# Hybrid attention and PEER block, 1 core: U and V rows gathered together, one-hot rows in groups of two

## Chip, cores and metric

One core of one Trainium2 chip runs the whole program. The metric is the device time of one execution in microseconds.

## Reference

One layer for 512 tokens of width 1024: a projection, latent attention and gated linear attention with an output projection, and then the part that the change is in, a retrieval from 16384 single-neuron experts (PEER):

```python
q = (hf @ w_q).reshape(T, PH, 2, PEER_HALF)
scores = jnp.einsum('thpd,hpnd->thpn', q, sub_keys, preferred_element_type=jnp.float32)
s, idx = lax.top_k(scores, K)
...
best, pos = lax.top_k(cand, K)
expert = jnp.take_along_axis(cand_idx, pos, axis=-1)
gate = jax.nn.softmax(best, axis=-1)
...
u = jnp.take(u_tab, eb, axis=0)
a = jax.nn.gelu(jnp.einsum('td,thkd->thk', xb, u, preferred_element_type=jnp.float32), approximate=False)
c = (a * gb).astype(h.dtype)
return jnp.einsum('thk,thkd->td', c, jnp.take(v_tab, eb, axis=0))
```

Each token picks 8 heads x 16 = 128 experts. It takes the dot product with each expert's row of U, a GELU and the gate, and the sum of the rows of V weighted by that.

## The kernel before

Products are made from fp32r halves: every operand x is split into hi (ScalarE copies it) and lo (x - hi, on DVE or POOL), and three matmuls hi*hi, lo*hi, hi*lo make one product.

The 512 tokens go two ways through the experts.

**The dense way, tokens 128 to 511 (ND = 384).** The 16384 experts are 128 blocks ("experts" below) of 128. For each of them the kernel makes U x (24 matmuls of 384 columns: 8 pieces of the width, three halves each), a GELU, a weight per expert and token (0 where the token did not pick it), and then C V (18 matmuls of 512 columns: 3 token blocks, 2 halves of the width, three halves each) into six PSUM banks. The weight comes from one-hot rows: `route(tt)` finds the picks of 128 tokens; `onehot(o)` builds for 8 tokens, on DVE and in f16, for each token a 128x128 row of ones at the first index (x1) and of the gate's hi and lo half at the second index (xh, xl); `spread(o)` multiplies them, two f16 matmuls per token, and ScalarE evicts them to `gs`, which goes to DRAM (`gd`) every 32 tokens. In the tiles x1, xh and xl of `[128, 2, 128, 4]` the innermost index is the token in a group of four, so the 128 columns of one token are four elements apart.

**The gathered way, tokens 0 to 127 (GT = 128).** One token per partition. For each of the 128 picks an indirect DMA on POOL's queue brings that token's row of U (4 KB), DVE takes the dot product in one pass (`scalar_tensor_tensor` with `accum_out`), after 32 picks ScalarE makes the GELU, and the rows of V are brought and added to `gout` in one DVE pass each. `gather()` is a generator of 256 steps that the other loops call.

**What sets the order.** The program runs in the order in which it is written; each engine takes its own instructions in that order. While `route` and `onehot` run on DVE, a planner fills TensorE with up-matmuls of the next experts. `Metered` adds a cost in ns for each instruction of PE and DVE, and `fill()` (L1187) calls `some(1)`, an eighth of an expert's up-matmuls, as long as PE's sum is behind DVE's. `gathered(G1)`, `gathered(GO)`, `gathered(GC)` advance the gather. Experts made so early go through DRAM (`gx` to `gad`, and back as `ga`); those that are left (`fresh`) are made between the steps of the down loop (L1383: `down`, `c_hi`, `v_hi`, `up_out`, `weigh`, `c_lo`, `v_lo`, `refill`, `up`, `gathering`) and stay in SBUF (`gf`). The lo half of a weight tile (wlo) is made by `lo_home[0]`, first POOL, and DVE from L952 on.

Of the kernel before, what the change touches and what calls it, by code (L numbers as in the profile page):

```python
# [10 lines left out]
F32 = mybir.dt.float32  # L11
# [11 lines left out]
D = 1024  # L23
# [8 lines left out]
NEG = -3.0e38  # L32
NA = 6
NF = 6
XAT = 120
# [4 lines left out]
P15 = 8  # L40
G1, GO = 0.25, 0.75
LEAD = 3000.0
# [9 lines left out]
ND = T - GT  # L52
GSL = 32
GC = 0.25
GBUF = 5
LEAVE = 8
# [38 lines left out]
def layout(x, positions, g_mix, w_in, g_q_lat, w_qb, g_kv_lat, w_kvb, w_a2, b_a2, g_gla, w_branch_a,  # L95
# [39 lines left out]
    a["u"] = ct(peer_u[0].reshape(128, 128, NC_D, 128).transpose(0, 3, 2, 1))  # L135
    a["ur"] = ct(peer_u[0])
    a["v"] = ct(peer_v[0].reshape(128, 128, D))
# [54 lines left out]
@with_exitstack
def body(ctx, tc, a, out):
# [757 lines left out]

    lo_home[0] = dve  # L952
    some(P15)
    product_keys(15)
    some(3 * NC_D - P15)
    ax = ExitStack()
    for tt in range(NT):
# [27 lines left out]
    gact = gp.tile([128, 128], F32, name="gact")  # L985
    NSB = 128 // GSL
    gsteps = [256]

    def gather():
        rows = {}  # L990
        src = [a["ur"], a["v"].rearrange("a b d -> (a b) d")]
        batches = [(0, 0)] + [x for b in range(NSB) for x in ([(0, b + 1)] if b + 1 < NSB else []) + [(1, b)]]
        work = [(v, GSL * b + j) for v, b in batches for j in range(GSL)]

        def fetch(n):
            if n < len(work):
                v, j = work[n]
                rows[n] = gp.tile([128, D], F32, name="rows", bufs=GBUF)
                pool.indirect_dma_start(out=rows[n], out_offset=None, in_=src[v],  # L999
                                        in_offset=bass.IndirectOffsetOnAxis(ap=gidx[:, j:j + 1], axis=0))  # L1000

        for n in range(GBUF - 2):
            fetch(n)
        yield
        for n, (v, j) in enumerate(work):
            fetch(n + GBUF - 2)
            r = rows.pop(n)
            gsteps[0] -= 1
            if v == 0:
                dve.scalar_tensor_tensor(r, r, 1.0, hrep, op0=OP.mult, op1=OP.mult, accum_out=gact[:, j:j + 1])  # L1010
                if j % GSL == GSL - 1:
                    b = slice(j + 1 - GSL, j + 1)
                    act.activation(gact[:, b], gact[:, b], AF.Gelu)
                    dve.tensor_tensor(gact[:, b], gact[:, b], ggat[:, b], op=OP.mult)
            else:
                dve.scalar_tensor_tensor(gout, r, gact[:, j:j + 1], gout, op0=OP.mult, op1=OP.add)
            yield
# [14 lines left out]
    NS = PH * TOPK  # L1032
    i1T, i2T, gh, gl = [pr.tile([128, T], F16, name=n) for n in ("i1T", "i2T", "gh", "gl")]
    TB = 32
    gd = dr.tile([128, T // TB, 128, TB], F32, name="gd")
    GS = 2.0 ** 15
    def route(tt):
# [4 lines left out]

        kx = pr.tile([128, 2, TOPK, PH, TOPK], F16, name="kx")
        d1 = pr.tile([128, PH, TOPK], F16, name="d1")
# [11 lines left out]
        pos = pr.tile([128, PH, TOPK], U32, name="pos")  # L1056
        wk = pr.tile([128, PH, NCAND], F32, name="cand2")
        for op in range(5):
            for hd in range(PH):
                x, y, b, i8 = cand[:, hd], wk[:, hd], best[:, hd], pos[:, hd]  # L1060
                if op == 0:
                    dve.max(b[:, 0:8], x)
                elif op == 1:
                    dve.max_index(i8[:, 0:8], b[:, 0:8], x)
                elif op == 2:
                    dve.match_replace(y, b[:, 0:8], x, NEG)
                elif op == 3:
                    dve.max(b[:, 8:16], y)
                else:
                    dve.max_index(i8[:, 8:16], b[:, 8:16], y)  # L1070
                if hd % 4 == 3:
                    if (op, hd) == K1:
                        act.activation(kx[:, 0], d1.rearrange("p h a -> p a h")[:, :, :, None].to_broadcast(spread_k), AF.Copy)
                    if (op, hd) == K2:
                        act.activation(kx[:, 1], fi[:, :, 1].rearrange("p h a -> p a h")[:, :, :, None].to_broadcast(spread_k), AF.Copy)
                    yield
# [7 lines left out]
        dve.tensor_copy(pf, pos.rearrange("p h k -> p (h k)"))  # L1084
        ge = pr.tile([128, TOPK, NS], F16, name="ge")
        m = pr.tile([128, 2, TOPK, NS], F16, name="m")
# [4 lines left out]
        def flat(x):  # L1091
            return x.rearrange("p a h k -> p a (h k)")

# [5 lines left out]
        dve.tensor_tensor(g, g, sm[:, 1, :, None].to_broadcast([128, PH, TOPK]), op=OP.mult)  # L1099
        dve.tensor_tensor(m[:, 0], ge, flat(kx[:, 0]), op=OP.mult)  # L1100
        yield
# [11 lines left out]
        yield  # L1113
        dve.tensor_tensor(m[:, 0], ge, flat(kx[:, 1]), op=OP.mult)
        n = TOPK // 2
        while n > 1:
            dve.tensor_tensor(m[:, 0, :n], m[:, 0, :n], m[:, 0, n:2 * n], op=OP.add)
            n //= 2
        yield
        dve.tensor_tensor(e2, m[:, 0, 0], m[:, 0, 1], op=OP.add)  # L1120
        for _ in range(6):
            yield
        if tt == 0:
# [3 lines left out]
            return  # L1127
        ts = slice(tt * 128, (tt + 1) * 128)
        p = pmm()
# [10 lines left out]
    def onehot(o):  # L1140

        full = [128, 2, 128, 4]
        it = iota[:, None].to_broadcast(full)
        t0 = 8 * o

        def col(x):
            return x[:, t0:t0 + 8].rearrange("p (g t) -> p g t", t=4)[:, :, None, :].to_broadcast(full)

        e1, e2, eh, el = [pr.tile([128, 2, 128, 4], F16, name=n, bufs=XB) for n in ("x1", "x2", "xh", "xl")]
        dve.tensor_tensor(e2, it, col(i2T), op=OP.is_equal)  # L1150
        (pool if o % 4 in PSH else dve).tensor_tensor(el, e2, col(gl), op=OP.mult)
# [27 lines left out]
    iota = pr.tile([128, 128, 4], F16, name="iota")  # L1179
    act.activation(iota, cc(C_IOTA, 128)[:, :, None].to_broadcast([128, 128, 4]), AF.Copy)  # L1180
    step = pr.tile([128, TOPK, NS], F16, name="step")
# [201 lines left out]
    for n in range(128 - ENDS):  # L1383
# [58 lines left out]
```

## Time and profile before

| | |
|---|---|
| median of 3 runs | 1702.72 us (1697.27 to 1703.1) |
| profiled execution, its own time | 1697.78 us |
| its span | 1695.9 us |
| PE busy | 1655.2 us, 8505 matmuls |
| DVE, ACT, POOL busy | 1263.6, 679.0, 575.9 us |
| DMA | 406.25 MB, 240 GB/s over the span |
| mean granted clock of TensorE | 0.993 |

The stages by time: projections, attention and the routing projection up to about 545 us; routing of the first tokens up to 632 us; one-hot products with up-matmuls beside them up to 905 us; the last early experts up to 950 us; the down loop up to 1657 us; the final norm up to the end. Matmuls are pipelined and overlap in the profile, so the time that one costs is the distance from its start to the next one's start. The granted clock is a share of full speed, 2.4 GHz; 0.50 is 1.2 GHz. Helpers record most operations under one line (L162), so groups are told apart by the names of the tiles, `out<-in`.

### The profile page before, as it was taken

What the parts mean: (1) busy time and instruction counts of PE and PEld (TensorE: products, weight loads), DVE (VectorE), ACT (ScalarE), POOL (GpSimd) and SP (SyncE); (2) the same over time, 40 slices, a digit from 0 to 9 for tenths busy, and PEclk for the clock granted to TensorE, in tenths of its full rate; (3) what the DMA queues carried; (4) which work ended last, traced back from release to release, by engine and by line L of the source; (5) the groups of instructions that cost most, each with busy time, mean ns of one, the idle gap of its engine ahead of it and who ended that gap; (6) DMA issues with size and microseconds to landing.
All of it is one profiled execution on the core that took longest, in us unless ns stands there. A gap on an engine that the chain in (4) does not pass through costs nothing.

```text
span 1695.9 us, 23253 instructions
## 1 busy us (share of the span) xinstructions
PE 1655.2 (98%) x8505; PEld 1445.6 (85%) x8505; DVE 1263.6 (75%) x2535; ACT 679.0 (40%) x999; POOL 575.9 (34%) x362
## 2 busy tenths in 40 slices
PE   7999999999998999999999999999999999999998
PEld 5777657888877999999999988888888888888887
DVE  6725575254889988989894677877788788878885
ACT  5442544244223635454444433333333333333333
POOL 4532233445330111111111243443454443454550
PEclk9999999999998999999999999999999999999999
DMA  5222113434232777787889999999999999999993
GB/s 173 66 74 72 52 67 132 141 130 149 88 100 88 250 242 235 262 274 260 278 299 344 330 313 325 324 338 328 305 371 331 341 365 328 319 364 324 336 332 131
DMA packets 168849, 406.25 MB, mean 240 GB/s; under 512 B 13383, under 2 KB 86216, under 8 KB 167072
## 3 DMA queue, kind: packets, MB, share of 16 engines
q1 hardware_dynamic: 118624, 230.09, 39.8%
q0 software_dynamic: 37008, 134.58, 22.8%
q10 hardware_dynamic: 13104, 40.11, 6.4%
q8 instruction: 66, 1.08, 0.3%
q14 instruction: 47, 0.39, 0.1%
HBM read 357.28 MB, written 47.45 MB: 239 GB/s over the span
## 4 chain that ended last, share of the span: by engine, by line
PE 85%; DVE 9%; issue 2%; ACT 2%; DMA 2%; POOL 0%; SPq 0%; DVEq 0%; POOLq 0%; ACTq 0%
PE pmm L162 54%; PE pk L162 17%; PE pst L162 14%; DVE kd L162 3%; DVE la L162 2%; DVE tmp L162 2%; DVE rB L162 1%; DMA raw<-in_w 1%; DMA gad<-gx 0%; DMA ga<-gad 0%; DVE r L162 0%; POOL wlo L241 0%; DVE act_lo L162 0%; ACT act_hi L322 0%; DVE stat L162 0%
## 5 line engine op out<-in xcount | busy, mean ns | idle before, releaser
L999 POOL DMA_INDIRECT rows<-in_ur,gidx x128 | 170.0, 1328 | 547.0 <-DVE rows L162 445.4
L162 PE MATMUL pmm<-act_hi,whi 128*128 128x384 f32 (+1 forms) x832 | 303.4, 365 | 12.0 <-ACT act_hi L327 8.7
L162 PE MATMUL pmm<-act_hi,wlo 128*128 128x384 f32 (+1 forms) x832 | 294.9, 354 | 8.5 <-DVE wlo L162 8.5
L162 PE MATMUL pmm<-act_lo,whi 128*128 128x384 f32 (+1 forms) x832 | 294.7, 354 | 0.5 <-DVE act_lo L162 0.5
L999 POOL DMA_INDIRECT rows<-in_v,gidx x128 | 205.4, 1605 | 215.3 <-DVE gout L162 172.2
L241 POOL TENSOR_TENSOR wlo<-raw,whi 128x1024 fp32r<-128x1024 f32 (+1 forms) x74 | 175.6, 2376 | 282.8 <-ACT whi L235 246.9
L235 ACT ACTIVATE whi<-raw 128x1024 fp32r<-128x1024 f32 (+1 forms) x202 | 209.6, 1038 | 109.4 <-PE pmm L162 61.9
L162 DVE TENSOR_TENSOR wlo<-raw,whi 128x1024 fp32r<-128x1024 f32 x128 | 156.3, 1222 | 109.5 <-ACT whi L235 109.5
L162 DVE TENSOR_TENSOR vlo<-vraw,vhi 128x1024 fp32r<-128x1024 f32 x128 | 156.3, 1221 | 82.3 <-issue 79.0
L162 PE MATMUL pmm<-vhi,chi 128*128 128x512 f32 x512 | 199.4, 389 | 0.0
L162 PE MATMUL pmm<-vhi,clo 128*128 128x512 f32 x512 | 199.2, 389 | 0.0
L162 PE MATMUL pmm<-vlo,chi 128*128 128x512 f32 x512 | 199.2, 389 | 0.0
L162 PEld LDWEIGHTS pmm<-act_hi,whi 128*128 128x128 f32 x832 | 159.7, 192 | 27.6 <-ACT act_hi L327 8.7
L162 PEld LDWEIGHTS pmm<-act_hi,wlo 128*128 128x128 f32 x832 | 158.7, 191 | 19.2 <-DVE wlo L162 9.5
L162 PEld LDWEIGHTS pmm<-act_lo,whi 128*128 128x128 f32 x832 | 159.1, 191 | 9.3 <-DVE act_lo L162 1.0
L162 DVE SCALAR_TENSOR_TENSOR gout<-rows,gact,gout 128x1024 f32<-128x1024 f32 x128 | 164.1, 1282 | 2.0 <-DMA rows<-in_v,gidx 0.2
L162 DVE SCALAR_TENSOR_TENSOR rows<-rows,hrep 128x1024 f32<-128x1024 f32 x128 | 153.4, 1219 | 0.5 <-DMA rows<-in_ur,gidx 0.5
L162 PE MATMUL pmm<-t,whi 128*128 128x512 f32 x448 | 141.8, 398 | 0.0
L162 PE MATMUL pk<-act_hi,wlo 128*128 128x384 f32 x416 | 139.1, 334 | 0.0
L162 PE MATMUL pk<-act_lo,whi 128*128 128x384 f32 x416 | 139.1, 334 | 0.0
L162 PE MATMUL pk<-act_hi,whi 128*128 128x384 f32 x416 | 139.0, 334 | 0.0
L1258 ACT ACTIVATE vhi<-vraw 128x1024 fp32r<-128x1024 f32 x128 | 133.9, 1048 | 0.8 <-ACT gx L974 0.5
(267 smaller groups left out, 2996.0 us busy)
## 6 DMA issues: line engine op xcount, KB each, us to landing
raw<-in_u SPq DMA_DIRECT2D x128, 512.0 KB, 4.7
vraw<-in_v SPq DMA_DIRECT2D x128, 512.0 KB, 6.7
gt<-gd SPq DMA_DIRECT2D x32, 768.0 KB, 8.5
gd<-gs ACTq DMA_DIRECT2D x11, 2048.0 KB, 7.2
gad<-gx ACTq DMA_DIRECT2D x76, 192.0 KB, 4.6
ga<-gad SPq DMA_DIRECT2D x76, 192.0 KB, 7.0
raw<-in_w SPq DMA_DIRECT2D x28, 512.0 KB, 3.3
raw<-in_wpq SPq DMA_DIRECT2D x16, 512.0 KB, 3.3
```

Source lines behind the costliest of these rows:

```text
L162: return f(*args, **kw)
L235: act.activation(hi[:, :n], raw[:, :n], AF.Copy)
L241: (lo_eng or lo_home[0]).tensor_tensor(lo[:, :n], raw[:, :n], hi[:, :n], op=OP.subtract)
L999: pool.indirect_dma_start(out=rows[n], out_offset=None, in_=src[v], in_offset=bass.IndirectOffsetOnAxis(ap=gidx[:, j:j + 1], axis=0))
L1258: act.activation(hi, vraw[n], AF.Copy)
```

## The change

- U and V are laid side by side in DRAM (`uv`, 8 KB a row). One indirect DMA brings both rows of a pick into a tile of `[128, 2048]`; there are 128 of them and 4 buffers, two fetched ahead, where there were 256 and 5. A step of the gather is now a dot product and, for the pick before, the sum. GELU and gate are two ScalarE instructions of one column per pick. The rates G1, GO and GC count steps of this kind.
- The one-hot tiles are `[128, 4, 128, 2]`: groups of two tokens, the columns of a token two elements apart.
- The planner counts an f16 matmul of n columns as n/2.4 + 4 ns (57.3 ns for 128) where it counted max(107, n/2.4) + 13 (120 ns).
- `lo_home` becomes DVE only after the first three experts' matmuls.
- SBUF is saved: route's m lies in kx and its second candidate tile in ge; x2 has one buffer; ga, gf five instead of six; clo three instead of four; gfin and the last rows' output use buffers that are there.

```diff
-NA = 6
-NF = 6
+NA = 5
+NF = 5
...
-G1, GO = 0.25, 0.75
+G1, GO = 0.125, 0.5
...
-GC = 0.25
-GBUF = 5
+GC = 0.125
+GBUF = 4
...
-    a["ur"] = ct(peer_u[0])
+    a["uv"] = np.concatenate([peer_u[0], peer_v[0]], axis=1)
...
+    if w.dtype == F16:
+        return n / 2.4 + 4.0
     return max(107.0, n / 2.4) + 13.0
...
-    lo_home[0] = dve
     some(P15)
     product_keys(15)
     some(3 * NC_D - P15)
+    lo_home[0] = dve
...
-            if n < len(work):
-                v, j = work[n]
-                rows[n] = gp.tile([128, D], F32, name="rows", bufs=GBUF)
-                pool.indirect_dma_start(out=rows[n], out_offset=None, in_=src[v],
-                                        in_offset=bass.IndirectOffsetOnAxis(ap=gidx[:, j:j + 1], axis=0))
+            if n < 128:
+                rows[n] = gp.tile([128, 2 * D], F32, name="rows", bufs=GBUF)
+                pool.indirect_dma_start(out=rows[n], out_offset=None, in_=a["uv"],
+                                        in_offset=bass.IndirectOffsetOnAxis(ap=gidx[:, n:n + 1], axis=0))
...
-        for n, (v, j) in enumerate(work):
-            fetch(n + GBUF - 2)
-            r = rows.pop(n)
+        for n in range(129):
             gsteps[0] -= 1
-            if v == 0:
-                dve.scalar_tensor_tensor(r, r, 1.0, hrep, op0=OP.mult, op1=OP.mult, accum_out=gact[:, j:j + 1])
-                if j % GSL == GSL - 1:
-                    b = slice(j + 1 - GSL, j + 1)
-                    act.activation(gact[:, b], gact[:, b], AF.Gelu)
-                    dve.tensor_tensor(gact[:, b], gact[:, b], ggat[:, b], op=OP.mult)
-            else:
-                dve.scalar_tensor_tensor(gout, r, gact[:, j:j + 1], gout, op0=OP.mult, op1=OP.add)
+            if n < 128:
+                fetch(n + GBUF - 2)
+                r, g = rows[n][:, :D], gact[:, n:n + 1]
+                dve.scalar_tensor_tensor(r, r, 1.0, hrep, op0=OP.mult, op1=OP.mult, accum_out=g)
+                act.activation(g, g, AF.Gelu)
+                act.activation(g, g, AF.Copy, scale=ggat[:, n:n + 1])
+            if n:
+                dve.scalar_tensor_tensor(gout, rows.pop(n - 1)[:, D:], gact[:, n - 1:n], gout, op0=OP.mult, op1=OP.add)
             yield
...
-        full = [128, 2, 128, 4]
+        full = [128, 4, 128, 2]
...
-            return x[:, t0:t0 + 8].rearrange("p (g t) -> p g t", t=4)[:, :, None, :].to_broadcast(full)
+            return x[:, t0:t0 + 8].rearrange("p (g t) -> p g t", t=2)[:, :, None, :].to_broadcast(full)
...
-                pe.matmul(p[:, i], eh[:, q, :, i], e1[:, q, :, i], start=True, stop=False)
-                pe.matmul(p[:, i], el[:, q, :, i], e1[:, q, :, i], start=False, stop=True)
+                g, t = 2 * q + i // 2, i % 2
+                pe.matmul(p[:, i], eh[:, g, :, t], e1[:, g, :, t], start=True, stop=False)
+                pe.matmul(p[:, i], el[:, g, :, t], e1[:, g, :, t], start=False, stop=True)
...
-            lo = dn.tile([128, ND], F32R, name="clo", bufs=CB)
+            lo = dn.tile([128, ND], F32R, name="clo", bufs=VL)
```

Three places of the order of instructions show what moves. The first is DVE at the end of `product_keys(15)` and the start of `route(0)` (la and cand are sorted scores and candidates, fi the indices), before:

```order
L162 MATCH_REPLACE tmp<-la,pk 128x128
L162 MAX la<-tmp 128x8
L162 MAX_INDEX kd<-la,tmp 128x8
L162 TENSOR_TENSOR wlo<-raw,whi 128x1024 x2
L162 TENSOR_SCALAR la<-la,r2c 128x256 x4
L162 CAST fi<-kd 128x256
```

and now:

```order
L161 MATCH_REPLACE tmp<-la,pk 128x128
L161 MAX la<-tmp 128x8
L161 MAX_INDEX kd<-la,tmp 128x8
L161 TENSOR_SCALAR la<-la,r2c 128x256 x4
L161 CAST fi<-kd 128x256
```

The two splits of weight tiles behind the searches, and one ahead of them, have left DVE; POOL has 19 in a row there instead of 16.

The second is ScalarE in the one-hot stage, one octet of tokens (gs evicts the one-hot products, gx is an early expert's GELU, whi a split). Before:

```order
L1168 ACTIVATE gs<-pk 128x128x4
L1168 ACTIVATE gs<-pst 128x128x4
L974 ACTIVATE gx<-pmm 128x384
L976 DMA gad<-gx 128x384
L235 ACTIVATE whi<-raw 128x1024
```

and now, with a gather step in the octet:

```order
L1162 ACTIVATE gs<-pk 128x128x4
L1162 ACTIVATE gs<-pst 128x128x4
L1008 ACTIVATE gact<-gact 128x1
L1009 ACTIVATE gact<-gact,ggat 128x1
L236 ACTIVATE whi<-raw 128x1024
L975 ACTIVATE gx<-pmm 128x384
L977 DMA gad<-gx 128x384
L236 ACTIVATE whi<-raw 128x1024
```

The GELU and the gate of one pick stand between the evictions and the next split, and there are more splits and early experts to an octet. Between the first and the last one-hot product PE has 1554 up-matmuls where it had 1038, and 96 experts go through DRAM instead of 76.

The third is DVE in the down loop, one step and the next. Before:

```order
L162 TENSOR_TENSOR ga<-ga,gt 128x384
L162 TENSOR_TENSOR clo<-ga,chi 128x384
L162 TENSOR_TENSOR vlo<-vraw,vhi 128x1024
L162 SCALAR_TENSOR_TENSOR rows,gact<-rows,hrep 128x1024 x2
L162 TENSOR_TENSOR gf<-gf,gt 128x384
```

and now:

```order
L161 TENSOR_TENSOR ga<-ga,gt 128x384
L161 TENSOR_TENSOR clo<-ga,chi 128x384
L161 TENSOR_TENSOR vlo<-vraw,vhi 128x1024
L161 TENSOR_TENSOR wlo<-raw,whi 128x1024
L161 SCALAR_TENSOR_TENSOR rows,gact<-rows,hrep 128x1024
L161 SCALAR_TENSOR_TENSOR gout<-rows,gact,gout 128x1024
```

Dot product and sum stand side by side in a step. The down loop has 101 dot products, 102 sums and 33 splits where it had 85, 128 and 54; in the one-hot stage there are 23 dot products, 23 sums and 66 splits where there were 35, none and 45.

## Rows read from the trace of the kernel before

**Rows 1.** The page's chain that ended last: shares of the span by engine.
```profile
PE 85%; DVE 9%; issue 2%; ACT 2%; DMA 2%; POOL 0%; SPq 0%; DVEq 0%; POOLq 0%; ACTq 0%
```

**Rows 2.** Table by stage: us, busy PE, PEld, DVE, ACT, POOL; clock, DMA, GB/s.
```profile
478.00:545.00 67.00, 56.66 (x279) 49.04 (x280) 61.95 (x312) 17.43 (x24) 14.40 (x6) 0.92 0.21 66
545.00:632.00 87.00, 87.00 (x505) 86.81 (x504) 78.79 (x306) 45.87 (x56) 12.22 (x10) 1.00 0.74 253
632.00:905.00 273.00, 273.00 (x1816) 264.86 (x1816) 244.56 (x534) 133.14 (x200) 41.04 (x36) 1.00 0.80 269
905.00:950.00 45.00, 43.30 (x250) 42.98 (x249) 17.15 (x20) 19.30 (x28) 2.25 (x3) 1.00 0.99 348
950.00:1657.00 707.00, 707.00 (x3404) 621.37 (x3403) 573.92 (x718) 252.78 (x349) 319.88 (x208) 1.00 0.95 334
```

**Rows 3.** The chain in order of time, down loop: start us, us, what.
```profile
1232.01 4.17 PE pk L162 x24
...
1240.26 2.72 PE pmm L162 x12
...
1244.34 2.72 PE pmm L162 x12
```

**Rows 4.** Timeline of PE over one octet: start us, us, engine, line, operation.
```profile
762.06 0.34 PE L162 MATMUL pmm<-act_hi,wlo 128*128 128x384 f32 x1
762.24 0.29 PE L162 MATMUL pk<-x,xh 128*128 128x128 f16 x1
...
764.05 0.42 PE L162 MATMUL pmm<-act_hi,whi 128*128 128x384 f32 x1
764.31 0.34 PE L162 MATMUL pmm<-act_lo,whi 128*128 128x384 f32 x1
```

**Rows 5.** Timeline of PE, three 256-column matmuls in a row.
```profile
88.13 0.28 PE L162 MATMUL pk<-whi,act_hi 128*128 128x256 f32 x1
88.24 0.28 PE L162 MATMUL pk<-wlo,act_hi 128*128 128x256 f32 x1
88.36 0.28 PE L162 MATMUL pk<-whi,act_lo 128*128 128x256 f32 x1
```

**Rows 6.** Groups of DVE instructions by form: busy us, mean ns, idle before.
```profile
L162 DVE TENSOR_TENSOR x<-iota,i2T 128x1024 f16<-128x1024 f16 x48 | 32.9, 685 | 0.0
L162 DVE TENSOR_TENSOR wlo<-raw,whi 128x1024 fp32r<-128x1024 f32 x128 | 156.3, 1222 | 109.5 <-ACT whi L235 109.5
L162 DVE SCALAR_TENSOR_TENSOR rows<-rows,hrep 128x1024 f32<-128x1024 f32 x128 | 153.4, 1219 | 0.5 <-DMA rows<-in_ur,gidx 0.5
L162 DVE SCALAR_TENSOR_TENSOR gout<-rows,gact,gout 128x1024 f32<-128x1024 f32 x128 | 164.1, 1282 | 2.0 <-DMA rows<-in_v,gidx 0.2
```

**Rows 7.** Waits of DVE, 950 to 1657 us: us in total, times, longest.
```profile
DVE vlo L162 <- issue: 73.3, 52, 3.1
DVE wlo L162 <- ACT whi L235: 53.1, 46, 1.3
```

**Rows 8.** DMA of 950 to 1657 us, and the stage table of 10 us.
```profile
DMA packets 110124, 235.93 MB, mean 334 GB/s; under 512 B 7648, under 2 KB 61613, under 8 KB 110079
...
1230.00:1240.00 10.00, 10.00 (x51) 8.98 (x50) 7.67 (x12) 2.41 (x4) 4.49 (x3) 1.00 1.03 401
```

**Rows 9.** Tile fin, ScalarE: one-column activations, ns min, median, max.
```profile
L1371 ACT ACTIVATE fin<-fin x4: 203/203/203, 1672.7 to 1690.0; 128x1 f32<-128x1 f32 x4
```

**Rows 10.** Stage table in steps of 5 us, and PE's longest wait around them.
```profile
525.00:530.00 5.00, 2.10 (x14) 1.49 (x12) 4.66 (x27) 1.06 (x1) 0.00 (x0) 0.98 0.00 0
530.00:535.00 5.00, 1.10 (x3) 1.10 (x4) 4.76 (x21) 0.00 (x0) 0.00 (x0) 0.50 0.03 8
535.00:540.00 5.00, 5.00 (x17) 5.00 (x17) 4.66 (x27) 0.00 (x0) 0.00 (x0) 0.50 0.30 97
...
PE pmm L162 <- DVE wlo L162: 6.8, 2, 6.6
```

**Rows 11.** Groups by form: the f16 weight load of the one-hot products.
```profile
L162 PEld LDWEIGHTS <-xl 128*128 128x128 f16 x384 | 45.5, 119 | 0.6
```

More of the change, by code (lines that the diff above doesn't have):

```diff
@@ L52 @@
 ND = T - GT
-GSL = 32
-GC = 0.25
-GBUF = 5
+GC = 0.125
+GBUF = 4
 LEAVE = 8
@@ L985, in body @@
     gact = gp.tile([128, 128], F32, name="gact")
-    NSB = 128 // GSL
-    gsteps = [256]
+    gsteps = [129]
     def gather():
         rows = {}
-        src = [a["ur"], a["v"].rearrange("a b d -> (a b) d")]
-        batches = [(0, 0)] + [x for b in range(NSB) for x in ([(0, b + 1)] if b + 1 < NSB else []) + [(1, b)]]
-        work = [(v, GSL * b + j) for v, b in batches for j in range(GSL)]
         def fetch(n):
-            if n < len(work):
-                v, j = work[n]
-                rows[n] = gp.tile([128, D], F32, name="rows", bufs=GBUF)
-                pool.indirect_dma_start(out=rows[n], out_offset=None, in_=src[v],
-                                        in_offset=bass.IndirectOffsetOnAxis(ap=gidx[:, j:j + 1], axis=0))
+            if n < 128:
+                rows[n] = gp.tile([128, 2 * D], F32, name="rows", bufs=GBUF)
+                pool.indirect_dma_start(out=rows[n], out_offset=None, in_=a["uv"],
+                                        in_offset=bass.IndirectOffsetOnAxis(ap=gidx[:, n:n + 1], axis=0))
         for n in range(GBUF - 2):
@@ L1032, in body @@
     NS = PH * TOPK
-    i1T, i2T, gh, gl = [pr.tile([128, T], F16, name=n) for n in ("i1T", "i2T", "gh", "gl")]
+    i1T, i2T, gh, gl = [pr.tile([128, ND], F16, name=n) for n in ("i1T", "i2T", "gh", "gl")]
     TB = 32
@@ L1041, in route @@
         fi = fi.rearrange("p (h s) k -> p h s k", s=2)
-        kx = pr.tile([128, 2, TOPK, PH, TOPK], F16, name="kx")
+        kx = pr.tile([128, 3, TOPK, PH, TOPK], F16, name="kx")
         d1 = pr.tile([128, PH, TOPK], F16, name="d1")
@@ L1056, in route @@
         pos = pr.tile([128, PH, TOPK], U32, name="pos")
-        wk = pr.tile([128, PH, NCAND], F32, name="cand2")
+        ge = pr.tile([128, TOPK, NS], F16, name="ge")
+        wk = ge.rearrange("p a n -> p (a n)")[:, :2 * PH * NCAND].bitcast(F32).rearrange("p (h n) -> p h n", n=NCAND)
         for op in range(5):
@@ L1072, in route @@
                     if (op, hd) == K1:
-                        act.activation(kx[:, 0], d1.rearrange("p h a -> p a h")[:, :, :, None].to_broadcast(spread_k), AF.Copy)
+                        act.activation(kx[:, 1], d1.rearrange("p h a -> p a h")[:, :, :, None].to_broadcast(spread_k), AF.Copy)
                     if (op, hd) == K2:
-                        act.activation(kx[:, 1], fi[:, :, 1].rearrange("p h a -> p a h")[:, :, :, None].to_broadcast(spread_k), AF.Copy)
+                        act.activation(kx[:, 0], fi[:, :, 1].rearrange("p h a -> p a h")[:, :, :, None].to_broadcast(spread_k), AF.Copy)
                     yield
@@ L1084, in route @@
         dve.tensor_copy(pf, pos.rearrange("p h k -> p (h k)"))
-        ge = pr.tile([128, TOPK, NS], F16, name="ge")
-        m = pr.tile([128, 2, TOPK, NS], F16, name="m")
+        m2 = kx[:, 0].rearrange("p a h k -> p a (h k)")
+        m = kx[:, 1:].rearrange("p s a h k -> p s a (h k)")
         e1 = pr.tile([128, NS], F32, name="e1")
@@ L1089, in route @@
         cb = pr.tile([128, NS], F16, name="cb")
-        def flat(x):
-            return x.rearrange("p a h k -> p a (h k)")
         for i in range(TOPK):
@@ L1099, in route @@
         dve.tensor_tensor(g, g, sm[:, 1, :, None].to_broadcast([128, PH, TOPK]), op=OP.mult)
-        dve.tensor_tensor(m[:, 0], ge, flat(kx[:, 0]), op=OP.mult)
+        dve.tensor_tensor(m[:, 0], ge, m[:, 0], op=OP.mult)
         yield
@@ L1113, in route @@
         yield
-        dve.tensor_tensor(m[:, 0], ge, flat(kx[:, 1]), op=OP.mult)
+        dve.tensor_tensor(m2, ge, m2, op=OP.mult)
         n = TOPK // 2
         while n > 1:
-            dve.tensor_tensor(m[:, 0, :n], m[:, 0, :n], m[:, 0, n:2 * n], op=OP.add)
+            dve.tensor_tensor(m2[:, :n], m2[:, :n], m2[:, n:2 * n], op=OP.add)
             n //= 2
         yield
-        dve.tensor_tensor(e2, m[:, 0, 0], m[:, 0, 1], op=OP.add)
+        dve.tensor_tensor(e2, m2[:, 0], m2[:, 1], op=OP.add)
         for _ in range(6):
@@ L1127, in route @@
             return
-        ts = slice(tt * 128, (tt + 1) * 128)
+        ts = slice(tt * 128 - GT, (tt + 1) * 128 - GT)
         p = pmm()
@@ L1140, in onehot @@
     def onehot(o):
-        full = [128, 2, 128, 4]
+        full = [128, 4, 128, 2]
         it = iota[:, None].to_broadcast(full)
-        t0 = 8 * o
+        t0 = 8 * o - GT
         def col(x):
-            return x[:, t0:t0 + 8].rearrange("p (g t) -> p g t", t=4)[:, :, None, :].to_broadcast(full)
-        e1, e2, eh, el = [pr.tile([128, 2, 128, 4], F16, name=n, bufs=XB) for n in ("x1", "x2", "xh", "xl")]
+            return x[:, t0:t0 + 8].rearrange("p (g t) -> p g t", t=2)[:, :, None, :].to_broadcast(full)
+        e1, e2, eh, el = [pr.tile([128, 4, 128, 2], F16, name=n, bufs=b) for n, b in (("x1", XB), ("x2", 1), ("xh", XB), ("xl", XB))]
         dve.tensor_tensor(e2, it, col(i2T), op=OP.is_equal)
@@ L1178, in body @@
     split_hi()
-    iota = pr.tile([128, 128, 4], F16, name="iota")
-    act.activation(iota, cc(C_IOTA, 128)[:, :, None].to_broadcast([128, 128, 4]), AF.Copy)
+    iota = pr.tile([128, 128, 2], F16, name="iota")
+    act.activation(iota, cc(C_IOTA, 128)[:, :, None].to_broadcast([128, 128, 2]), AF.Copy)
     step = pr.tile([128, TOPK, NS], F16, name="step")
@@ L1364, in finish @@
         f = fin[:, row]
-        o = dn.tile([128, D], F32, name="vraw", bufs=VB)
+        o = gp.tile([128, 2 * D], F32, name="rows", bufs=GBUF)[:, :D]
         for d, x in enumerate(halves):
@@ L1397, in body @@
             x2v = [sb.tile([128, 1024], F32, name="raw", bufs=3).rearrange("p (c t) -> p c t", t=128) for _ in range(NBK)]
-            gfin = dn.tile([128, D], F32, name="gfin")
             for b in range(NBK):
                 sp.dma_start(x2v[b], x2d[:, :, b * 128:(b + 1) * 128])
+        if n == XAT + 3:
+            gfin = dn.tile([128, D], F32, name="vraw", bufs=VB)
             sp.dma_start(gfin, bass.AP(tensor=a["gfin"].tensor, offset=a["gfin"].offset, ap=[[0, 128], [1, D]]))
```

## The prediction

> **What bounds the kernel now.** I read the chain that ended last first: 85% of it is TensorE [rows 1], so what counts is TensorE's time and where it stands still. Then a table by stage [rows 2]. From 545 us to 1657 us TensorE is busy in all but 2 us, at the full granted clock, so there a microsecond of TensorE work is a microsecond of run time. DVE is close behind (245 of 273 us while the one-hot products are made, 574 of 707 us in the down loop), and in the down loop the DMA engines stand at 0.95. Before 545 us there is one real hole: in the first row of that group PE has 56.7 of 67 us and a clock of 0.92.
>
> Busy time hides what one matmul costs, since they overlap, so I take the distance from start to start. In the chain an expert's 24 up-matmuls of 384 columns take 4.17 us, 174 ns each, and a step of the down loop with 18 matmuls of 512 columns takes 4.08 us from start to start, 227 ns each [rows 3]. At 2.4 GHz (the granted clock is 1.00) 384 and 512 columns are 160 and 213 ns, so some 13.5 ns come on top. The 16 one-hot matmuls of an octet of tokens run from 762.24 us to 764.31 us, less one 384-column matmul: 1.90 us, 118.5 ns each [rows 4], although their 128 columns are only 53.3 ns.
>
> **The change part by part.** *One-hot rows in groups of two.* The two f16 operands of a one-hot matmul are now read with a step of two elements (4 bytes) instead of four (8 bytes). 118.5 ns is twice 53.3 plus 11.9, as if the moving operand came at half rate; the fp32r operands, whose columns lie 4 bytes apart, come at one column per clock [rows 3]. With the same 4 bytes the f16 product should cost 53.3 ns plus the extra of the nearest row, which is the shortest: 256 columns start every 0.115 us [rows 5], 8 ns over their 106.7 ns. I take 62 ns. The bounds are 53.3 ns (nothing on top; the changed planner itself prices it 57.3) and 118.5 ns (nothing gained); a shorter step gives no reason for a loss. There are 384 tokens with two matmuls each, 768: 768 x 56.5 ns = **-43.4 us**, bounds -50.1 and 0. All of it lies on TensorE in the full stretch 632 to 905 us.
>
> A rule of the skill speaks against this. The Trainium skill, "SBUF — State Buffer", says under its port map that SBUF has lines of 16 bytes and that two accesses to a line already give full bandwidth; the old 8-byte step has two. The Trainium skill, "TensorE: Matmul & The Clock Gate" (LDWEIGHTS), gives a weight load columns / 1.2 GHz, 107 ns for 128 columns at any step. By the two together this term is 0 and the sum 1696. The f16 loads of this trace, 119 ns each [rows 11], agree with the second; whether the first holds for TensorE no run here shows.
>
> *What the planner makes of it.* It now counts 63 ns less for each of the 768 matmuls and puts more experts' up-projections beside the one-hot work: by the order of the instructions 64.75 experts' matmuls lie between the first and the last one-hot product instead of 43.25, and 96 instead of 76 experts go out to DRAM and come back, leaving 32 instead of 52 to the down loop. The matmuls are the same at the same 174 ns, so on TensorE this moves 83 us from the down loop to the one-hot stage and costs nothing, as long as DVE and DMA keep up in both.
>
> DVE in the one-hot stage: 21 more splits of 1.22 us (25.6), and for 35 dot products of 1.22 us now 23 of these and 23 sums of 1.28 us [rows 6], 14.9 us more: 244.6 + 25.6 + 14.9 = 285 us. TensorE there: 64.75 x 4.17 + 768 x 0.062 = 318 us. DVE has 33 us to spare, so I count 0. In the down loop DVE loses 21 splits and 26 sums and gains 16 dot products: 573.9 - 25.6 - 33.3 + 19.5 = 535 us of about 624, and its 53 us of waits for ACT's half of a split shrink with the splits. Before, it spent 73 us waiting for nothing that the profile names ahead of vlo [rows 7], slack by its place. I count 0.
>
> DMA in the down loop: 235.9 MB [rows 8] less 20 U tiles (10.5), plus 20 stored activations (3.9), less 10 gathered half-rows (5.2): 224 MB in 624 us, 359 GB/s. The rows show 401 GB/s over 10 us [rows 8] with TensorE full, but only 348 in the stretch from 905 to 950 us, where the DMA engines stand at 0.99 [rows 2]. At 348 the loop would last 644 us, so the bounds are 0 and +20 us. I take **0**, since the demand is below what was delivered while TensorE ran on; the other end is a rival.
>
> *The gather.* One 8 KB row in place of two 4 KB rows: as many bytes, 128 issues on POOL instead of 256, and nobody but the gather waits for POOL there. DVE does the same 256 passes. New are 256 one-column activations; the nearest row has 0.203 us for one [rows 9], 52 us on ACT, which is busy 133 of 273 us and 253 of 707 us [rows 2]. They stand in ACT's queue ahead of the next evictions and splits and wait for DVE's dot product; DVE's own sum of 1.28 us follows that product, and ACT is through its two in 0.4 us, so DVE does not meet the wait. Behind them wait TensorE's evictions and the weight splits, which have two and three buffers. 0; without that cover at most the 52 us, spread over 1100 us.
>
> *Splits on POOL for longer.* The wlo splits at the end of the routing projection leave DVE. Between 525 and 540 us TensorE issues 14 + 3 + 17 matmuls [rows 10] where 86 fit: 52 x 0.174 = 9.1 us are lost, 6.6 of them in one wait for a wlo that DVE has queued behind the top-16 searches, and the rest at a granted clock of 0.50 (1.2 GHz) after that pause. The three splits go to POOL, which stands idle there. TensorE then runs ahead of DVE, and the next splits are on DVE again, so not all of it need last: at least the 3.7 us of which DVE is relieved, at most 9.1. DVE has 8 us unbusy in the next 87 [rows 2] to catch up, so I take **-6.5 us**.
>
> *The rest* (smaller buffers, shared tiles, where gfin and the last rows lie) frees SBUF. It makes a stored activation start its return one expert later and lets clo wait where vlo waited. With the slack above: 0.
>
> **Sum** against the profiled execution of 1697.8 us: -43.4 - 6.5 = 1647.9. The median of the three runs is 4.9 us above that execution, so I give 1653.
>
> **Rivals.** *A, the forecast:* about 1653, own range 1640 to 1670.
> *B, the down loop falls to DMA.* The stretches without an up-projection are longer now, and in each of them a step of 4.08 us wants 0.52 MB of V, 0.2 of weights, 0.2 of activations and 0.87 of gathered rows, 438 GB/s, above the 401 seen. For it: 0.95 busy already. Against: buffers bridge such stretches today without a stop. Price up to 20 us: 1660 to 1675.
> *C, the step changes nothing.* What TensorE waits for would be the weight load, not the moving operand: the f16 load takes 119 ns [rows 11], as long as the distance between two matmuls, and no row shows a 128-column load in much less. Against: the 384-column matmuls hide their loads. Then only the stall goes: 1697.8 - 6.5 + 4.9 = 1696, and up to 20 more if B joins. By the two rules of the skill cited above it is this case that comes.
> *D, the other side: DVE's one-hot passes.* Their innermost run is two elements long now. They take 0.685 us for 1024 f16 elements, a pass over 1024 fp32 elements 1.22 us [rows 6]. If the short run costs the packed rate, 192 passes take 0.54 us more each, 103 us, and DVE needs 388 us against TensorE's 318: +70 us, 1723. It decides as soon as a pass costs over 0.172 us more (33 us over 192). Against: a run of two f16 still fills 4 bytes; for: no row shows a run that short.
>
> **How the numbers follow.** A 0.60, B 0.16, C 0.12, D 0.07, and 0.05 for other things, such as ACT held at the new small activations. What a measurement of this kernel can tell from no change is 0.5%, some 8.5 us. A and B are faster, and a little of C and of the rest: 0.79. Most of C is no change: 0.10. D, C with B, and half of the rest are slower: 0.11. The range takes in A with its bounds, B, and the lower edge of C: 1640 to 1690.
>
> **What would show it.** Start to start of the one-hot matmuls: near 62 ns for A, 118 for C. The passes on DVE at 0.685 us, or over 0.85 for D. No TensorE hole and no clock of 0.50 around 530 us. The one-hot stage near 318 us and the down loop near 624; a down loop of 640 and waits of DVE or ACT for vraw, ga or rows would be B. The prediction is wrong if the spacing falls and the time does not.

## The result and the profile after

The changed kernel takes 1653.07 us (median of 4 runs, 1650.91 to 1654.97), the kernel before, on the same chip, 1702.80 us: a ratio of 0.9715 with a 95% interval of 0.9691 to 0.9739, or 48.5 us less (44 to 53). The forecast was 1653. The profiled execution is the 1650.91 us one, span 1649.1 us.

The chain that ended last, shares by engine, against [rows 1]:

```profile
PE 83%; DVE 9%; DMA 2%; issue 2%; ACT 2%; POOL 0%; ACTq 0%; SPq 0%; DVEq 0%; POOLq 0%
```

The bound is the same engine. The table by stage, with the columns of [rows 2] but cut where the stages now begin and end: the first one-hot product starts at 623.4 us and the last at 940.9, the first product with V starts at 986.5.

```profile
478.00:545.00 67.00, 60.31 (x314) 52.68 (x314) 61.59 (x322) 19.73 (x26) 21.59 (x9) 0.99 0.30 98
545.00:623.40 78.40, 78.40 (x449) 78.21 (x448) 69.73 (x281) 41.93 (x55) 5.66 (x5) 0.99 0.67 238
623.40:941.00 317.60, 317.60 (x2330) 310.43 (x2329) 286.71 (x560) 167.88 (x289) 25.05 (x24) 1.00 0.85 300
941.00:986.00 45.00, 43.03 (x250) 42.72 (x248) 18.71 (x21) 19.55 (x30) 0.94 (x1) 1.00 1.02 363
986.00:1610.00 624.00, 623.61 (x2914) 535.76 (x2913) 524.84 (x696) 266.07 (x505) 101.25 (x98) 1.00 0.96 355
```

The down loop is shown up to 1610 us, as far from the end as 1657 us was before. The one-hot stage holds more work than before and is longer (317.6 us), the down loop is shorter (624 us), and TensorE is busy in both. The time came out of single matmuls. Timeline of PE over one octet, as [rows 4]:

```profile
767.37 0.23 PE L161 MATMUL pk<-x,xh 128*128 128x128 f16 x1
767.44 0.22 PE L161 MATMUL pk<-x,xl 128*128 128x128 f16 x1
...
768.25 0.22 PE L161 MATMUL pst<-x,xl 128*128 128x128 f16 x1
768.27 0.42 PE L161 MATMUL pmm<-act_hi,whi 128*128 128x384 f32 x1
768.53 0.34 PE L161 MATMUL pmm<-act_lo,whi 128*128 128x384 f32 x1
```

From 767.37 to 768.53 us, less one 384-column matmul of 0.174: 0.986 us for 16, **61.6 ns** each where it was 118.5. Times 768 that is 43.7 us. Groups by form, as [rows 6] and [rows 11]:

```profile
L161 DVE SCALAR_TENSOR_TENSOR gout<-rows,gact,gout 128x1024 f32<-128x1024 f32 x128 | 164.2, 1283 | 0.0
...
L996 POOL DMA_INDIRECT rows<-in_uv,gidx x128 | 132.9, 1038 | 935.9 <-DVE gout L161 884.7 <-PE pmm L161 45.3 <-DVE clo L161 4.9
...
L161 PEld LDWEIGHTS <-xl 128*128 128x128 f16 x384 | 37.4, 97 | 0.0
...
L161 DVE TENSOR_TENSOR x<-iota,i2T 128x1024 f16<-128x1024 f16 x48 | 32.9, 685 | 0.0
...
L1008 ACT ACTIVATE gact<-gact 128x1 f32<-128x1 f32 x128 | 26.0, 203 | 197.8 <-DVE rows L161 197.7
```

DVE's one-hot passes take the same 685 ns with runs of two, and a sum the same 1.28 us. The small activation takes the 203 ns that it was priced at. POOL issues one indirect DMA per pick and mostly waits for buffers. The f16 weight load fell from 119 to 97 ns, and the products now follow each other in 61.6 ns, well under one load.

The rest is the hole ahead of the routing. By 620 us, before any one-hot product, TensorE has started 2837 matmuls where it had started 2808: 29 x 0.174 = 5.0 us gained. Stage table up to 620 us, before and now:

```profile
0.00:620.00 620.00, 588.24 (x2808) 477.71 (x2809) 397.55 (x1189) 257.28 (x390) 212.69 (x116) 0.98 0.35 119
...
0.00:620.00 620.00, 592.04 (x2837) 481.68 (x2838) 396.93 (x1200) 259.96 (x398) 212.91 (x114) 0.99 0.36 120
```

Stage table in 5 us steps, against [rows 10]:

```profile
535.00:540.00 5.00, 3.75 (x22) 3.43 (x20) 4.76 (x25) 1.55 (x2) 0.00 (x0) 1.00 0.12 27
540.00:545.00 5.00, 2.44 (x10) 2.12 (x10) 4.52 (x23) 3.72 (x6) 0.00 (x0) 0.89 0.97 332
545.00:550.00 5.00, 5.00 (x24) 5.00 (x24) 2.68 (x29) 5.00 (x4) 0.00 (x0) 0.77 0.54 182
```

The hole is smaller and has moved 10 to 15 us later; it did not close. The longest wait in it is now 2.3 us, where it was 6.6.

### The profile page after: what moved, and what is told of

It reads as the page before. It is cut to its first block, busy times and chain, and to the rows that moved or that the text cites. A ratio compares the mean times of both kernels' runs of the same rounds, so it can differ in the third digit from the quotient of the medians.

```text
span 1649.1 us, 23157 instructions
## 1 busy us (share of the span) xinstructions
PE 1611.3 (98%) x8505; PEld 1400.6 (85%) x8505; DVE 1251.9 (76%) x2528; ACT 727.9 (44%) x1251; POOL 340.1 (21%) x237
## 3 DMA queue, kind: packets, MB, share of 16 engines
q0 software_dynamic: 18576, 134.57, 21.7%
## 4 chain that ended last, share of the span: by engine, by line
PE 83%; DVE 9%; DMA 2%; issue 2%; ACT 2%; POOL 0%; ACTq 0%; SPq 0%; DVEq 0%; POOLq 0%
PE pmm L161 59%; PE pst L161 13%; PE pk L161 11%; DVE kd L161 3%; DVE la L161 2%; DVE tmp L161 2%; DMA ga<-gad 1%; DMA gad<-gx 1%; DVE rB L161 0%; DVE r L161 0%; DVE act_lo L161 0%; ACT whi L236 0%; POOL wlo L242 0%; DVE rows L161 0%; DMA raw<-in_w 0%
## 5 line engine op out<-in xcount | busy, mean ns | idle before, releaser
L161 PE MATMUL pmm<-act_hi,whi 128*128 128x384 f32 (+1 forms) x992 | 355.5, 358 | 12.9 <-ACT act_hi L328 8.1
L161 PE MATMUL pmm<-act_hi,wlo 128*128 128x384 f32 (+1 forms) x992 | 347.6, 350 | 4.3 <-DVE wlo L161 4.3
L161 PE MATMUL pmm<-act_lo,whi 128*128 128x384 f32 (+1 forms) x992 | 347.3, 350 | 0.5 <-DVE act_lo L161 0.5
L996 POOL DMA_INDIRECT rows<-in_uv,gidx x128 | 132.9, 1038 | 935.9 <-DVE gout L161 884.7
L161 PEld LDWEIGHTS pmm<-act_hi,whi 128*128 128x128 f32 x992 | 188.4, 190 | 28.5 <-ACT act_hi L328 8.1
L161 PEld LDWEIGHTS pmm<-act_hi,wlo 128*128 128x128 f32 x992 | 188.1, 190 | 14.5 <-DVE wlo L161 4.9
L161 PEld LDWEIGHTS pmm<-act_lo,whi 128*128 128x128 f32 x992 | 188.4, 190 | 9.3 <-DVE act_lo L161 1.0
L161 PEld LDWEIGHTS pmm<-vlo,chi 128*128 128x128 f32 x512 | 96.1, 188 | 22.8 <-DVE vlo L161 2.9
L161 PEld LDWEIGHTS pmm<-vhi,clo 128*128 128x128 f32 x512 | 96.1, 188 | 18.7
L161 PEld LDWEIGHTS pmm<-vhi,chi 128*128 128x128 f32 x512 | 96.1, 188 | 18.6
```

Of the source, the lines that this page charges most:

```text
L161: return f(*args, **kw)
L996: pool.indirect_dma_start(out=rows[n], out_offset=None, in_=a["uv"], in_offset=bass.IndirectOffsetOnAxis(ap=gidx[:, n:n + 1], axis=0))
```

## Experiments

Twelve kernels were run. Ratios are to the kernel before, run beside each of them (its median was 1699.3 to 1699.4 us). e5 to e8 were run once each, so for them only the time stands, with 1700.1 us for the kernel before beside it.

### The two halves of the one-hot term: layout and planner

**e1: the changed kernel with groups of four.**

```diff
-        full = [128, 4, 128, 2]
+        full = [128, 2, 128, 4]
...
-                g, t = 2 * q + i // 2, i % 2
+                g, t = q, i
```

> The changed kernel with the one-hot tiles back in groups of four tokens; planner's price, gather and splits as changed. If the step between a token's columns sets the f16 matmul (forecast), start to start goes from 62 back to 118.5 ns and the time rises by 768 x 56.5 = 43 us, to 1697 (1692 to 1702), with TensorE full in the one-hot stage. If the gain comes from the planner's new fill or from the joint gather, the time stays near 1653 to 1660.

Measured: 1696.40 us (10 runs), ratio 0.9977 (0.9965 to 0.9989). Everything but the layout is worth about 4 us together, of which the splits on POOL give 3.4 by themselves (e11); without the layout the planner's new price saves nothing that shows. The f16 products and their loads are as long as before the change. Groups by form:

```profile
L161 PE MATMUL pk<-x,xl 128*128 128x128 f16 x192 | 48.3, 297 | 0.0
...
L161 PEld LDWEIGHTS <-xl 128*128 128x128 f16 x384 | 45.4, 118 | 0.6
```

**e2: the kernel before with groups of two, nothing else.** The edit is the reverse of e1's, made in the kernel before.

> The kernel before with nothing changed but the one-hot tiles in groups of two. Step theory: start to start 62 ns. But the planner still puts only 43.25 experts beside the one-hot work, so TensorE needs 43.25 x 4.17 + 768 x 0.062 = 228 us there and DVE 245 us and more: the stage becomes DVE's, TensorE waits, and only 272 - 250 = 22 us or so of the 43 come out: 1680 (1674 to 1686). If DVE's order does not bind after all: 1659. If the step changes nothing: 1703.

Measured: 1675.95 us, ratio 0.9862 (0.9847 to 0.9877), 23.5 us less. The matmuls are nearly as short as in the changed kernel (recorded with 222 to 225 ns, there with 218 to 222, and in the kernel before with 297), and yet some 20 of the 43.7 us do not arrive. TensorE's waits from 615 to 960 us (us in total, times, longest):

```profile
PE pk L162 <- DVE x L162: 9.5, 5, 2.7
PE pmm L162 <- DVE wlo L162: 6.6, 4, 3.0
```

TensorE, faster than the planner believes, runs out of up-matmuls and waits for DVE, 16 us in all. In the kernel before it waited 1.7 us in the same stretch, in the changed kernel not at all.

**e3: the changed kernel with the planner's old price.**

```diff
-    if w.dtype == F16:
-        return n / 2.4 + 4.0
```

> The changed kernel with the planner's old price for f16 matmuls (120 ns). 80 experts instead of 96 are made early, 48.25 of them beside the one-hot work: TensorE 48.25 x 4.17 + 48 = 249 us there, DVE about 265. If the new price is what lets TensorE keep the gain: TensorE waits in that stage and the time is 1666 to 1674. If TensorE's matmuls alone count: 1653, within 4 us.

Measured: 1679.67 us, ratio 0.9883 (0.9868 to 0.9898), 26.6 us above the changed kernel by the medians. The direction was right, the loss larger than the 13 to 21 us expected. TensorE's waits, 615 to 960 us:

```profile
PE pmm L161 <- DVE wlo L161: 12.2, 4, 8.0
PE pk L161 <- DVE x L161: 7.0, 5, 2.0
PE pk L161 <- ACT gx L973: 6.7, 4, 2.3
```

They sum to 26 us, about the loss; in e2 they were 16 us and the loss about 20 (e2 is 23.4 us above e12, below, and 3.4 of these are the splits on POOL). The two halves need each other: the layout frees TensorE time, and the price sees that up-matmuls are put there.

### What the f16 matmul waits for

Four kernels, run once each, separate the step of the moving operand (x1) from that of the weights (xh, xl). Each builds the tiles with their own group size, as in

```diff
-        e1, e2, eh, el = [pr.tile([128, 4, 128, 2], F16, name=n, bufs=b) for n, b in (("x1", XB), ("x2", 1), ("xh", XB), ("xl", XB))]
...
+        e1 = pr.tile(shape(4), F16, name="x1", bufs=XB)
+        e2, eh, el = [pr.tile(shape(2), F16, name=n, bufs=b) for n, b in (("x2", 1), ("xh", XB), ("xl", XB))]
```

where `shape(n)` is `[128, 8 // n, 128, n]`.

**e5: weights in groups of two, moving operand in groups of four.**

> The changed kernel with only the stationary tiles (xh, xl) in groups of two, the moving one (x1) in groups of four. If the moving operand's step set the pace (as the forecast put it): start to start 118 ns, 1697. If the weight load's step did: 62 ns, 1653. If either alone is enough to slow it: 118 here and in the next run.

Measured: 1698.93 us. One octet on PE:

```profile
708.77 0.28 PE L161 MATMUL pk<-x,xh 128*128 128x128 f16 x1
...
710.81 0.33 PE L161 MATMUL pmm<-act_lo,whi 128*128 128x384 f32 x1
```

(2.04 - 0.174) / 16 = 117 ns: nothing gained. The load of its weights by form:

```profile
L161 PEld LDWEIGHTS <-xl 128*128 128x128 f16 x384 | 43.5, 113 | 0.2
```

These weights have the same 4-byte step as in the changed kernel, where the load is recorded with 97 ns. So the recorded length of a load does not follow the step of the weights alone.

**e6: weights in groups of four, moving operand in groups of two.**

> The mirror: stationary tiles in groups of four, the moving one in groups of two. Moving step sets the pace: 62 ns, 1653. Weight step: 118 ns, 1697. Either alone: 118 ns.

Measured: 1658.96 us. One octet on PE, and the load of its weights by form:

```profile
702.15 0.25 PE L161 MATMUL pk<-x,xh 128*128 128x128 f16 x1
...
703.36 0.34 PE L161 MATMUL pmm<-act_lo,whi 128*128 128x384 f32 x1
```

```profile
L161 PEld LDWEIGHTS <-xl 128*128 128x128 f16 x384 | 44.3, 115 | 0.0
```

(1.21 - 0.174) / 16 = 65 ns, with loads of 115 ns. So the pace is the moving operand's, and a weight load nearly twice as long as the spacing is hidden. The weights' step is worth 3 ns a matmul, some 2.5 us; the other 3 us of this one run are within what runs of one kernel differ by (4 us for the changed kernel, up to 8 for others).

**e7: all in groups of eight, a step of 16 bytes.** To make room, route's `cb` shares `pf`'s tile.

> The changed kernel with groups of eight, a step of 16 bytes in both operands, so that each column of a token lies in a 16-byte line of its own (cb shares pf's tile to make room). If the rate halves with each doubling of the step: start to start some 225 ns, 768 x 163 = 125 us more, 1778. If half rate is the floor: 118 ns, 1697. If lines of 16 bytes with two hits were what matters (the page's rule), the loss would begin only here.

Measured: 1810.21 us. One octet on PE, and one stretch of the stage table:

```profile
707.23 0.43 PE L161 MATMUL pk<-x,xh 128*128 128x128 f16 x1
...
711.18 0.34 PE L161 MATMUL pmm<-act_lo,whi 128*128 128x384 f32 x1
```

```profile
624.00:1100.00 476.00, 476.00 (x2320) 406.72 (x2319) 288.72 (x560) 172.59 (x289) 25.04 (x24) 0.93 0.58 202
```

(3.95 - 0.174) / 16 = 236 ns, twice the 118.5 again. Against the changed kernel 768 x 174 ns = 134 us would give 1787; the remaining 23 us go with the granted clock, which is 0.93 in the mean over this stage although PE is busy throughout. After 19 of the 48 octets it falls to its lower level, though TensorE has waited for nothing, and the 384-column matmuls then start 320 ns apart, 384 columns at 1.2 GHz, where 174 ns is usual. One such stretch, first in the timeline and then in the stage table:

```profile
638.59 0.53 PE L161 MATMUL pmm<-act_hi,wlo 128*128 128x384 f32 x1
638.91 0.53 PE L161 MATMUL pmm<-act_hi,whi 128*128 128x384 f32 x1
...
638.00:641.50 3.50, 3.50 (x14) 3.48 (x13) 1.08 (x6) 2.04 (x3) 0.00 (x0) 0.53 0.19 69
```

**e8: one token at a time, a step of 2 bytes.**

> The changed kernel with each token's columns side by side, a step of 2 bytes, so DVE's passes have an innermost run of one element. TensorE: 53 to 62 ns, nothing more to gain (0 to -7 us) if 4 bytes are already full rate. DVE, rival D's mechanism: passes of 0.685 us if the run does not matter, then 1646 to 1655; 1.22 us if a run of one loses the packed rate, then DVE needs 388 us in that stage against TensorE's 318 and the time is near 1723, with TensorE waiting for DVE's one-hot tiles.

Measured: 1737.66 us. One octet on PE:

```profile
701.02 0.23 PE L161 MATMUL pk<-x,xh 128*128 128x128 f16 x1
...
702.16 0.34 PE L161 MATMUL pmm<-act_lo,whi 128*128 128x384 f32 x1
```

(1.14 - 0.174) / 16 = 60.4 ns: below 4 bytes TensorE gains hardly more (1.2 ns a matmul). DVE's pass by form, and TensorE's waits from 615 to 1010 us:

```profile
L161 DVE TENSOR_TENSOR x<-iota,i2T 128x1024 f16<-128x1024 f16 x48 | 58.4, 1217 | 0.0
```

```profile
PE pmm L161 <- DVE wlo L161: 26.7, 19, 3.5
PE pk L161 <- DVE x L161: 23.3, 10, 3.7
```

With a run of one the pass takes 1217 ns, as an fp32 pass does. In this layout iota and the result lie side by side, and the token's own operand is one value repeated over the 128 columns. DVE is busy for 385 of 392 us, and TensorE waits 50 us for it (its granted clock there is 0.97). Rival D's mechanism is real; it begins at a run of one and not of two.

### The gather

**e4: the changed kernel with two indirect DMAs of 4 KB into the same tile.**

```diff
...
-                pool.indirect_dma_start(out=rows[n], out_offset=None, in_=a["uv"],
-                                        in_offset=bass.IndirectOffsetOnAxis(ap=gidx[:, n:n + 1], axis=0))
+                for i, tab in enumerate((a["ur"], a["v"].rearrange("a b d -> (a b) d"))):
+                    pool.indirect_dma_start(out=rows[n][:, i * D:(i + 1) * D], out_offset=None, in_=tab,
+                                            in_offset=bass.IndirectOffsetOnAxis(ap=gidx[:, n:n + 1], axis=0))
```

> The changed kernel with two indirect DMAs of 4 KB rows into the halves of the same tile in place of one of 8 KB rows: 256 issues on POOL. Forecast: the joint row is worth nothing, 1653 within 3 us. If larger rows relieve the DMA engines in the down loop: 1660 to 1675, with DMA waits of DVE or ACT in the loop.

Measured: 1652.06 us, ratio 0.9717 (0.9704 to 0.9731), the changed kernel's own. The joint row is worth nothing here.

**e12: the kernel before with groups of two, the new price and the splits on POOL, without the new gather and without the smaller buffers.**

> The kernel before with three parts of the change: groups of two tokens, the planner's new price, and wlo splits on POOL for longer. Not in it: the rows side by side, the sum a slot behind the dot product, the 256 small activations, and all that saves SBUF. The prediction put those at 0 in sum: then this is 1653, as the changed kernel, ratio 0.971. If the dot products and sums side by side, or DVE's lighter load in the one-hot stage (there are 35 dot products there with the old gather, 23 dot products and 23 sums with the new), matter, it comes out otherwise: DVE would be relieved by some 15 us in that stage, which is worth nothing if TensorE bounds it; a loss of over 4 us would show that the gather's new form has a worth of its own, through the waits of the down loop.

Measured: 1652.58 us, ratio 0.9729 (0.9715 to 0.9743). That is the changed kernel's time with the old gather. TensorE is as full there (one-hot stage and down loop in the cut of [rows 2]):

```profile
632.00:905.00 273.00, 273.00 (x2008) 266.62 (x2008) 244.63 (x523) 137.22 (x212) 36.13 (x32) 1.00 0.83 286
...
950.00:1610.00 660.00, 657.38 (x3115) 571.08 (x3114) 554.99 (x704) 234.73 (x323) 341.46 (x208) 1.00 0.99 356
```

The old gather keeps POOL busy for 341 us of the loop; DVE, which uses its rows, waits 0.5 us for one.

### The splits on POOL

**e11: the kernel before with this move alone.**

```diff
-    lo_home[0] = dve
     some(P15)
     product_keys(15)
     some(3 * NC_D - P15)
+    lo_home[0] = dve
```

> The kernel before with one line moved: the wlo splits stay on POOL until the first three experts' matmuls are written. If the hole between 525 and 545 us is worth what the opposite edit took from the changed kernel (4.7 us by the medians, 1657.8 to 1653.1), this is 3 to 6 us faster than the kernel before: 1694 to 1697, ratio 0.997. If the work only comes earlier, and DVE, which is the slower engine in the one-hot stage of the kernel before too, takes it back, the ratio is 1.000.

Measured: 1696.14 us (12 runs), ratio 0.9980 (0.9971 to 0.9988): 3.4 us, 2 to 5. By 620 us it has started 2830 matmuls, 22 more than the kernel before: 3.8 us.

**e9: the changed kernel with the move undone.**

> The changed kernel with one line moved back: the wlo splits go to DVE from before the last piece of the routing projection on, as before the change. If the term of the hole is right (TensorE had issued 29 more up-matmuls by 620 us with the change, 29 x 0.174 = 5.0 us), this is 3 to 6 us slower than the changed kernel's 1653.1: 1656 to 1659, and TensorE again has one wait of over 6 us for a wlo between 525 and 545 us. If those matmuls were only brought forward and the time is taken up later (rival), the time stays at 1653.

Measured: 1657.79 us (1652.49 to 1659.85), ratio 0.9743 (0.9722 to 0.9764). The median is 4.7 us above the changed kernel's, but the two intervals overlap, so these runs alone do not tell the two kernels apart; the trace has 18 matmuls fewer by 620 us, 3.1 us. The old hole is back. Stage table, and PE's longest wait from 500 to 620 us:

```profile
525.00:530.00 5.00, 0.46 (x4) 0.14 (x2) 4.69 (x27) 0.00 (x0) 0.00 (x0) 0.92 0.00 0
530.00:535.00 5.00, 2.92 (x9) 2.92 (x10) 4.73 (x21) 0.00 (x0) 0.00 (x0) 0.50 0.28 105
```

```profile
PE pmm L161 <- DVE wlo L161: 7.8, 2, 6.6
```

**e10: four experts on POOL instead of three**, to close the rest of the hole.

```diff
-    some(3 * NC_D - P15)
+    some(4 * NC_D - P15)
```

> The changed kernel, but the wlo splits become DVE's only after the first four experts' matmuls instead of three. What is left of the hole in the changed kernel is waits of TensorE for a wlo of DVE of 2.3 us at most and some 10 us at a granted clock of 0.77 to 0.89 between 535 and 550 us, 3 us or so of lost work. If DVE's share of the splits keeps TensorE waiting there, one expert more on POOL gives 1 to 3 us: 1650 to 1652. If DVE, busy over 0.9 of the stretch, is late anyway, or POOL's split with its longer pass becomes the wait, no change or a loss: 1653 to 1656.

Measured: 1655.08 us (1654.35 to 1657.13), ratio 0.9735 (0.9718 to 0.9752): no gain. Stage table:

```profile
535.00:540.00 5.00, 5.00 (x30) 5.00 (x29) 4.69 (x25) 1.88 (x3) 2.40 (x1) 1.00 0.30 95
540.00:545.00 5.00, 4.83 (x28) 4.51 (x28) 4.79 (x30) 2.01 (x4) 0.00 (x0) 1.00 0.39 104
545.00:550.00 5.00, 5.00 (x31) 5.00 (x30) 1.78 (x7) 0.49 (x1) 0.00 (x0) 1.00 0.93 338
550.00:555.00 5.00, 4.36 (x24) 3.78 (x24) 3.90 (x32) 4.99 (x5) 0.00 (x0) 1.00 0.42 149
555.00:632.00 77.00, 75.07 (x441) 73.95 (x440) 69.30 (x260) 40.67 (x55) 6.25 (x5) 1.00 0.65 238
```

The hole at 535 to 550 us is filled, and new ones stand behind it (550 to 632 us has 465 matmuls, in the changed kernel 488); by 620 us 2825 are started, 12 fewer. None of the variants beats the changed kernel by more than the runs differ.

## Why the prediction was right, step by step

*One-hot matmuls, -43.4 us.* Forecast 62 ns, measured 61.6; -43.7 us. That the moving operand's step sets the pace was an assumption, and e5 and e6 show it: that step alone gives 117 or 65 ns, while the weights' step hardly matters. How the 62 ns were made up was luck in part. The working adds 8 ns to each matmul; inside an octet the extra is about half of that (14 steps from 767.44 to 768.25 us, 58 ns each), and the rest, some 0.06 us an octet, lies at its two ends.

Rival C had a weight load in the way; a load of 97 to 115 ns lies hidden under products 62 to 65 ns apart. The trace before the change already spoke against C: the 384-column matmuls of [rows 3] start 174 ns apart, and each of their weight loads is recorded with 188 ns.

```profile
L162 PEld LDWEIGHTS pk<-act_hi,whi 128*128 128x128 f32 x416 | 78.1, 188 | 1.9
```

The rule of the Trainium skill, "SBUF — State Buffer" (port map), that two accesses to a line of 16 bytes give full bandwidth, does not hold for this operand: two f16 of a line (8-byte step) cost twice what four cost, and one costs almost four times as much (e7).

*The planner, 0 us.* As a cost that was right: DVE 286.7 of 317.6 us in the one-hot stage, forecast 285 of 318; in the down loop 524.8 of 624, forecast 535 of 624. What the working does not say is that the first term depends on it. Without the price only some 23 of the 43 us arrive (e2), with everything else in place the loss is 27 (e3). The sum counted the price as a harmless move; it is half of the gain.

*DMA in the down loop, 0 us.* Forecast 359 GB/s in 624 us, measured 355, with DMA at 0.96. TensorE's waits in this stretch are 0.2 us. Rival B did not come, though its signs are there among the waits of other engines, 986 to 1610 us:

```profile
DVE ga L161 <- DMA ga<-gad: 14.5, 6, 7.4
...
ACT vhi L1252 <- DMA vraw<-in_v: 23.0, 14, 4.2
```

These were absorbed by slack. How much more traffic the loop would bear was not tried.

*Gather and small activations, 0 us.* Right for the time (e4, e12). The working names ScalarE's wait for the dot product without a size, and it is not small: 180.5 us in 95 waits of up to 4.1 us in the loop, since a GELU stands in its queue ahead of other work:

```profile
ACT gact L1008 <- DVE rows L161: 180.5, 95, 4.1
```

That hides behind its slack (266 of 624 us busy), as TensorE's 0.2 us of waits show.

*Splits on POOL, -6.5 us (3.7 to 9.1).* The right mechanism, its term too large: 3.4 us alone (e11), 5.0 us by the count of matmuls in the changed kernel, 3.1 by that of e9. The step that failed is the guess that DVE would catch up within the next 87 us: from 535 to 545 us it is still busy for 4.5 to 4.8 of every 5 us, and TensorE waits 2.3 us for a wlo. The hole partly moves behind the POOL splits, and e10 shows that it moves again if POOL takes one more.

The measured parts give -43.7 - 3.4 = -47.1 of the 48.5 us (44 to 53), where the working has -49.9. That the median still meets the forecast to 0.1 us is luck: the POOL term is some 3 us too large, and the 1702.8 us of the kernel before, a median of 4 runs, are 3 us above its medians beside the experiments (9 to 17 runs each). Against those, e4 and e12, which have the changed kernel's time, save 46.8 to 47.3 us.

## To carry to other kernels

Look at the step in bytes of TensorE's moving operand in f16: 4 bytes or less ran at nearly one column per clock here, 8 at half and 16 at a quarter of that, while the weights' step hid behind the products. Look at the engine that writes the tile in the same layout: at a step of 2 bytes DVE lost far more than TensorE gained (e8). When a kernel is filled by a planner that counts costs, correct the price together with the layout: either alone gave half of the gain or none. Bringing two rows by one DMA was worth nothing here, though it halved the issues, since hardly anyone had waited for that queue.

## Not expected of the hardware

- 128 f16 columns every 60.4, 61.6, 118.5 and 236 ns at steps of 2, 4, 8 and 16 bytes. The weight loads, with both operands at the same step, grew far less: about 100, 97, 116 to 119 and 145 to 148 ns. With the weights at 4 bytes and the moving operand at 8 they are 113 to 115 (e5).
- f16 products with a new set of 128 weights each follow each other in 61.6 ns, though the load of one set is recorded with 97 ns.
- In e7 PE is busy throughout the one-hot stage and its granted clock is 0.93 in the mean, where it is 1.00 at a step of 4 or 8 bytes. It falls to 1.2 GHz right behind 19 of the 48 octets, that is, after 16 of these slow f16 products in a row. What sets it was not tried.
- A DVE f16 pass with an innermost run of two keeps 685 ns per 1024 elements; with a run of one (one operand a single value repeated) it takes 1217.
- The gather's queue moved 134.57 MB in 18576 packets instead of 134.58 MB in 37008, and took 21.7% of the DMA engines' span instead of 22.8%: half as many packets saved hardly any time.
